# A hybrid decoder layer on one core: the projection's left operand turned by DMA instead of by TensorE

## The chip, the cores and the metric

The kernel runs on one core of a Trainium2 chip. The metric is the device time of one execution in microseconds (us). Each kernel is timed as the median of several executions, and one further execution was recorded by the hardware profiler; the rows shown here come from that recorded one. Engines are named as the profile names them: PE is TensorE, DVE is VectorE, ACT is ScalarE, POOL is GpSimd, SP is SyncE, which here only issues transfers. SPq in a row is SP's queue.

## The reference

One decoder layer over 4096 tokens of width 1024, in float32. The input is normed and projected to 2816 columns; 8 heads of windowed attention (window 128, with a sink and a slope per head) and 4 heads of a chunked linear recurrence run side by side on them. Each of the two gives 512 columns per token:

```python
attn = rmsnorm(swa_sink_alibi(q_a, k_a, v_a, attn_sinks[l]), attn_out_norm[l])
hg = hgrn2(q_h, f_h, i_h, lb_all[l])
hg = rmsnorm(hg, hgrn_out_norm[l].reshape(HGRN_HEADS, HGRN_VAL_DIM)).reshape(B, T, HGRN_WIDTH)
hg = hg * jax.nn.silu(g_h)
mix = jnp.concatenate([attn, hg], axis=-1) @ w_out[l]
x = x + ga1 * rmsnorm(mix, ln1_post[l])
```

Behind it stand a second norm, a router (4 groups, 8 experts in each, 2 experts per token) and the 32 experts' feed-forward, whose result is added to x after one more norm. The change concerns the operand of `@ w_out`, the "mixed heads".

## The kernel before

The kernel has three stages. The first sweep (to about 970 us of the trace) projects the tokens in 16 blocks of 256, runs the recurrence and leaves its 512 columns of each 128-token tile in DRAM (`hg_d`). The second sweep (about 970 to 1820 us) goes over 32 tiles of 128 tokens, two in a block: `g_qkv` projects queries, keys and values of a block, `g_attn` is the attention of one tile, `g_out` multiplies the mixed heads of one tile by `w_out`, `g_post` norms, adds, and makes the router's operand `h2T`, `g_route` routes four tiles at a time. The third stage runs the experts.

Products with a float32 operand are made of float16 halves: a value is scaled and split into a high part (rounded to float16) and a low part (the rest), and three matmuls, high by high, high by low and low by high, are summed in PSUM. The left operand of a matmul must lie transposed. In `g_out` (lines 1354 to 1386) the left operand is `mT`, 8 pieces of 128 columns with two halves each, so that a tile takes 2 x 8 x 3 = 48 matmuls of 128 x 512.

How `mT` is made before the change stands at the end of `g_attn` (lines 1336 to 1352). The tile's `mix` is 128 tokens x 1024 columns in float32: columns 0 to 511 are written by the attention, columns 512 to 1023 are loaded from `hg_d` at the beginning of `g_attn`. For each half of the columns TensorE turns four pieces of 128 x 128 in float32 into PSUM (`ps_t<-ident,mix`); ScalarE writes the scaled high half from PSUM, VectorE the low half. The recurrence's half goes first, the attention's half after its norm factor `r`, which VectorE multiplies in (`mix<-mix,rar`).

The order of the work is not written out by hand. `Weave` runs these functions as coroutines and keeps a model of the engines' clocks; it takes the next step of the first one whose operands should be there. So each engine's program, and SP's queue too, is the order in which the steps came up in that model, and it is fixed when the kernel is built. All loads and stores of the second sweep are issued by SP in that order, and SP waits at each transfer for what the transfer needs. `g_attn` of tile n starts once `mT` of tile n-2 was made (line 1237), and `mT` (two buffers) may be written once `g_out` of tile n-2 has ended (line 1341). One kind of DMA transpose is in the kernel already: `g_post` has SP turn the split router operand (`h2T<-x`, 128 x 2048 float16, 512 KB, 30 of them).

Of the kernel before, what the change touches and what calls it, by code (L numbers as in the profile page):

```python
# [9 lines left out]
F32 = mybir.dt.float32  # L10
F16 = mybir.dt.float16
FR = mybir.dt.float32r
BF = mybir.dt.bfloat16
# [3 lines left out]
AF = mybir.ActivationFunctionType  # L17
ALU = mybir.AluOpType
# [3 lines left out]
P = 128  # L22
D = 1024
KC = D // P
# [131 lines left out]
WAIT = "wait"  # L156
# [116 lines left out]
class Layer:  # L273
# [842 lines left out]
    def g_wo(self):  # L1116
# [4 lines left out]
        wo = self.wo = wp.tile([P, KC, 2, D], F16, name="w")  # L1121
# [20 lines left out]
    def sweep2(self, w16a):  # L1142
# [7 lines left out]
        with ExitStack() as ctx:  # L1150
# [23 lines left out]
            wr = op.tile([P, KC, 36], F32, name="mT")  # L1174
# [59 lines left out]
            def g_attn(n):  # L1234

                b, t = divmod(n, 2)
                while n >= 2 and ("mT", n - 2) not in st or ("q", b) not in st or n and ("s", n - 1) not in st:
                    yield WAIT
                qT, qv = st["q", b]
                mix = op.tile([P, D], F32, name="mix")  # L1240
                nc.sync.dma_start(mix[:, 512:], self.hg_d[n])
# [64 lines left out]
                mixa = mix[:, 0:512].rearrange("p (h d) -> p h d", d=64)  # L1306
# [29 lines left out]
                ss = sm.tile([P, 1], F32, name="ssa")  # L1336
                nc.scalar.activation(s[:, 0:2].rearrange("p h n -> p (h n)"), mix[:, 0:512], AF.Square,
                                     accum_out=ss)
                yield
                r = self.rstd(sm, ss, 1, 512, "ra")  # L1340
                while "const" not in st or n >= 2 and ("y", n - 2) not in st:
                    yield WAIT
                mT = op.tile([P, KC, 2, P], F16, name="mT")
                for kk in (1, 0):
                    if not kk:
                        yield [r]
                        nc.vector.tensor_scalar_mul(mix[:, 0:512], mix[:, 0:512], r)
                        yield
                    yield [mix, "ps_t"]
                    pt = ps_t.tile([P, 4, P], F32, name="ps_t")  # L1350
                    for k in range(4):
                        nc.tensor.transpose(pt[:, k], mix[:, (4 * kk + k) * P:(4 * kk + k + 1) * P], self.ident)
                    hi, lo2 = mT[:, 4 * kk:4 * kk + 4, 0], mT[:, 4 * kk:4 * kk + 4, 1]
                    nc.scalar.activation(hi, pt, AF.Copy, scale=osc[:, 1:2])
                    nc.vector.scalar_tensor_tensor(lo2, pt, osc[:, 1:2], hi, op0=ALU.mult, op1=ALU.subtract)
                st["mT", n] = mT

            def g_out(n):
                while ("mT", n) not in st or (n >= 3 and ("h2T", n - 3) not in st):
                    yield WAIT  # L1360
                mT = st["mT", n]
# [6 lines left out]
                yield [mT]  # L1368
                ym = xp.tile([P, D], F32, name="x", bufs=3)
                ss = sm.tile([P, 2], F32, name="ssy")  # L1370
                for c in range(2):
                    pj = ps_j.tile([P, 512], F32, name="ps_j")
                    for k in range(KC):
                        while ("wo", k) not in st:
                            yield WAIT
                        for i, (u, v) in enumerate(((0, 0), (0, 1), (1, 0))):
                            nc.tensor.matmul(pj, mT[:, k, v], wo[:, k, u, c * 512:(c + 1) * 512],
                                             start=(k == 0 and i == 0), stop=(k == KC - 1 and i == 2))
# [7 lines left out]
            def g_post(n):  # L1386
# [21 lines left out]
                if late:  # L1408
                    junk = op.tile([P, D], F32, name="mix")
# [911 lines left out]
```

## Time and profile before

| | |
|---|---|
| median of 3 runs (lowest, highest) | 2713.15 us (2712.32 to 2718.62) |
| the profiled execution: time, span | 2708.02 us, 2706.2 us |
| busy over the span | PE 92%, DVE 71%, ACT 50%, POOL 28% |
| second sweep, 1000 to 1800 us: busy | PE 95.4%, DVE 82.0%, ACT 55.5%, POOL 30.0% |
| second sweep: mean share of the 16 DMA engines | 0.45 |
| instructions on PE, matmuls | 19433 |

The span is the time from the first to the last instruction; the execution's own time lies 1.8 us above it. A row of groups gives the number of instructions, their busy time and the mean of one in nanoseconds, then the time that the engine sat idle just before them and what ended it. Matmuls are pipelined: the mean of one is its latency, so for a row of them the distance from one group's start to the next says more than the mean. All work is recorded under one line (L140, a helper), so groups are told apart by the names of their tiles.

### The profile page before, as it was taken

To read this page: it belongs to the slowest core of one execution; us is meant where nothing else is said; L and a number is where in the kernel's file an instruction comes from. 1 tells how busy PE (TensorE), PEld (TensorE's weight loads), DVE (VectorE), ACT (ScalarE), POOL (GpSimd) and SP (SyncE) were. 2 spreads that over 40 slices of the span, in tenths; PEclk is the share of its full clock that TensorE was granted. 3 is DMA by queue.
4 is the path that set the end of the run, shared out by engine and by line. 5 is a ranking of instruction groups with operands and counts; after the bars stand their busy time and mean duration, and the time that the engine had idled before them with its cause. 6 is when DMAs were issued, how large, how long until landed. Compare 5 with 4: busy or idle time off the path is not lost. (4 is left out here: it accounts for less than half of the span.)

```text
span 2706.2 us, 50271 instructions
## 1 busy us (share of the span) xinstructions
PE 2495.3 (92%) x19433; PEld 1908.5 (71%) x19433; DVE 1908.4 (71%) x4115; ACT 1360.0 (50%) x2932; POOL 758.8 (28%) x1075
## 2 busy tenths in 40 slices
PE   5989999999999989999999999975999989999992
PEld 2767667767766775766676667645998878888982
DVE  5657656787777678878788788884655656666774
ACT  4435544333433346546554655543555556666662
POOL 1111212211111001232332333334442333233336
PEclk8999999999999999999999999987999999999996
DMA  8212222222222243344446436536756878788988
GB/s 284 90 61 79 94 79 75 65 89 92 75 69 85 85 166 102 112 93 125 95 112 131 95 110 114 91 126 177 253 191 230 266 249 291 279 269 291 325 277 234
DMA packets 190602, 414.46 MB, mean 153 GB/s; under 512 B 85052, under 2 KB 120040, under 8 KB 168856
## 3 DMA queue, kind: packets, MB, share of 16 engines
q1 hardware_dynamic: 157360, 319.07, 37.8%
q0 software_dynamic: 31744, 91.60, 11.7%
q8 instruction: 153, 2.51, 0.4%
q14 instruction: 89, 0.73, 0.1%
q10 hardware_dynamic: 1256, 0.56, 0.1%
HBM read 284.60 MB, written 118.16 MB: 149 GB/s over the span
## 5 line engine op out<-in xcount | busy, mean ns | idle before, releaser
L140 PE MATMUL ps_g<-xT,w 128*128 128x256 f32 (+8 forms) x3072 | 465.5, 306 | 0.0
L140 PEld LDWEIGHTS ps_g<-xT,w 128*128 128x128 f32 x3072 | 436.1, 190 | 7.1 <-DVE xT L140 0.3
L140 PE MATMUL ps_j<-w,mT 128*128 128x512 f16 x1536 | 364.1, 381 | 0.0
L140 PE MATMUL ps_j<-hT,w 128*128 128x256 f16 x3072 | 348.7, 274 | 5.2 <-POOL hT L140 5.2
L140 PE MATMUL ps_j<-w,hT 128*128 128x512 f16 x1536 | 349.5, 380 | 0.0
L140 PEld LDWEIGHTS <-w 128*128 128x128 f16 x3072 | 301.8, 98 | 47.2 <-issue 8.7
L140 PEld LDWEIGHTS <-hT 128*128 128x128 f16 x2304 | 194.5, 98 | 164.0 <-issue 3.3
L140 PE MATMUL ps_d<-w,av 128*128 128x512 f32 (+6 forms) x1020 | 261.5, 401 | 4.6 <-ACT av L140 4.3
L140 ACT ACTIVATE w<-ws 128x512 fp32r<-128x512 f32 (+1 forms) x392 | 246.2, 678 | 29.7 <-DMA ws<-in_w_in_dram 25.1
L140 DVE TENSOR_TENSOR w<-ws,w 128x512 fp32r<-128x512 f32 x384 | 245.2, 685 | 2.1 <-ACT w L140 2.0
L140 PEld LDWEIGHTS <-mT 128*128 128x128 f16 x1536 | 143.3, 98 | 146.0 <-issue 8.6
L140 DVE TENSOR_TENSOR xT<-ps_x,xT 128x256 fp32r<-128x256 f32 (+8 forms) x256 | 115.2, 472 | 160.7 <-ACT xT L140 160.4
L140 PE MATMUL ps_j<-hT,w16a 128*128 128x256 f16 x1920 | 223.7, 276 | 0.0
L140 PEld LDWEIGHTS ps_d<-w,av 128*128 128x128 f32 (+6 forms) x1020 | 175.6, 178 | 53.8 <-ACT av L140 6.9
L140 PEld LDWEIGHTS <-w16a 128*128 128x128 f16 x1920 | 188.7, 99 | 26.4 <-issue 0.6
L140 POOL TENSOR_TENSOR hT<-hf,hT 128x512 f16<-128x512 f32 x64 | 103.6, 1619 | 269.8 <-ACT hT L140 255.3
L140 ACT ACTIVATE y<-ps_d,wgt 128x512 f32<-128x512 f32 (+4 forms) x141 | 97.1, 689 | 115.6 <-PE ps_d L140 92.1
L140 ACT ACTIVATE xT<-ps_x 128x256 fp32r<-128x256 f32 (+8 forms) x256 | 101.0, 422 | 103.7 <-PE ps_x L140 102.7
L140 ACT ACTIVATE s<-s,mx,qsc 128x256 f32<-128x256 f32 (+1 forms) x256 | 148.9, 584 | 0.0
L140 PE MATMUL ps_x<-ident,xg 128*128 128x128 f32 (+7 forms) x680 | 123.5, 289 | 26.7 <-DMA xg<-h_d,tok 16.0
L140 POOL DMA_INDIRECT xg<-h_d,tok x85 | 87.5, 1030 | 207.2 <-PE ps_x L140 187.7
L140 PEld LDWEIGHTS ps_x<-ident,xg 128*128 128x128 f32 (+7 forms) x680 | 104.6, 192 | 50.9 <-DMA xg<-h_d,tok 19.1
(405 smaller groups left out, 4243.4 us busy)
## 6 DMA issues: line engine op xcount, KB each, us to landing
ws<-in_w_exp_gate_dram SPq DMA_DIRECT2D x32, 1024.0 KB
ws<-in_w_exp_up_dram SPq DMA_DIRECT2D x32, 1024.0 KB
ws<-in_w_exp_down_dram SPq DMA_DIRECT2D x32, 1024.0 KB
yy<-y_d SPq DMA_DIRECT2D x24, 1024.0 KB
x<-in_x_dram SPq DMA_DIRECT2D x32, 512.0 KB
hT_d<-hT SPq DMA_DIRECT2D x16, 1024.0 KB
m_w<-in_w_ada_dram SPq DMA_DIRECT2D x128, 128.0 KB
hT<-hT_d SPq DMA_DIRECT2D x16, 1024.0 KB
```

The lines of the kernel that those rows point to most:

```text
L140: r = f(*a, **kw)
```

## The change

`mT` becomes two tiles of three buffers, `mT0` for the attention's half and `mT1` for the recurrence's. Each half is split while it still lies token by token: ScalarE writes the high part and VectorE the low part, both from SBUF, into 128 x 1024 float16 (`halves`), and SP turns that in one DMA transpose of 256 KB. The factor `r` is multiplied with the scale in one 128 x 1 operation (`rm`) and comes in as the scale of the split. The recurrence's half no longer lies in `mix`: it is loaded into `rec` and split by a coroutine of its own, `g_rec`. `halves` and `rec` lie in the half of the slot of `w` that `wo` does not take, which is free after the first sweep. `g_attn` of tile n now starts once `mT0` of n-3 and `mT1` of n-2 were made, and `g_out` takes the recurrence's pieces (4 to 7) first.

```diff
-        wo = self.wo = wp.tile([P, KC, 2, D], F16, name="w")
+        w = wp.tile([P, 2, KC * 2 * D], F16, name="w")
+        wo = self.wo = w[:, 0].rearrange("p (k u n) -> p k u n", k=KC, u=2)
+        self.halves = [[w[:, 1, c * D:(c + 1) * D].rearrange("p (u n) -> p u n", u=2) for c in (2 * i, 2 * i + 1)]
+                       for i in range(2)]
+        self.rec = [w[:, 1, c * D:(c + 1) * D].bitcast(F32) for c in (4, 5)]
...
-                while n >= 2 and ("mT", n - 2) not in st or ("q", b) not in st or n and ("s", n - 1) not in st:
+                while (n >= 3 and ("mT", n - 3, 0) not in st or n >= 2 and ("mT", n - 2, 1) not in st
+                       or ("q", b) not in st or n and ("s", n - 1) not in st):
...
-                mix = op.tile([P, D], F32, name="mix")
-                nc.sync.dma_start(mix[:, 512:], self.hg_d[n])
+                mix = op.tile([P, 512], F32, name="mix", bufs=3)
+                rec = self.rec[n % 2]
+                nc.sync.dma_start(rec, self.hg_d[n])
+                wv.add(g_rec(n, rec))
...
-                mT = op.tile([P, KC, 2, P], F16, name="mT")
-                for kk in (1, 0):
-                    if not kk:
-                        yield [r]
-                        nc.vector.tensor_scalar_mul(mix[:, 0:512], mix[:, 0:512], r)
-                        yield
-                    yield [mix, "ps_t"]
-                    pt = ps_t.tile([P, 4, P], F32, name="ps_t")
-                    for k in range(4):
-                        nc.tensor.transpose(pt[:, k], mix[:, (4 * kk + k) * P:(4 * kk + k + 1) * P], self.ident)
-                    hi, lo2 = mT[:, 4 * kk:4 * kk + 4, 0], mT[:, 4 * kk:4 * kk + 4, 1]
-                    nc.scalar.activation(hi, pt, AF.Copy, scale=osc[:, 1:2])
-                    nc.vector.scalar_tensor_tensor(lo2, pt, osc[:, 1:2], hi, op0=ALU.mult, op1=ALU.subtract)
-                st["mT", n] = mT
+                rm = sm.tile([P, 1], F32, name="rm", bufs=3)
+                nc.vector.tensor_mul(rm, r, osc[:, 1:2])
+                yield from turn(0, n, mix, rm)
+
+            def turn(i, n, x, scale):
+
+                while n >= 2 and ("mT", n - 2, i) not in st:
+                    yield WAIT
+                hl = self.halves[i][n % 2]
+                yield [scale, "Activation"]
+                nc.scalar.activation(hl[:, 0], x, AF.Copy, scale=scale)
+                yield
+                nc.vector.scalar_tensor_tensor(hl[:, 1], x, scale, hl[:, 0], op0=ALU.mult, op1=ALU.subtract)
+                while n >= 3 and ("y", n - 3) not in st:
+                    yield WAIT
+                yield
+                mT = op.tile([P, 2, 4, P], F16, name="mT%d" % i, bufs=3)
+                nc.sync.dma_start_transpose(mT.rearrange("p u k n -> p (u k) n"), hl.rearrange("p u n -> p (u n)"))
+                st["mT", n, i] = mT
```

In TensorE's program of before, in the middle of the second sweep, the four transposes of a half of the mixed heads stand between the projection's matmuls (`ps_j<-w,mT`) of an older tile and the transposes of the attention's weights `s`:

```order
L140 LDWEIGHTS mT
L140 MATMUL ps_j<-w,mT 128x512
L140 MATMUL ps_t<-ident,mix 128x128 x4
L140 MATMUL ps_t<-ident,s 128x128 x4
L140 LDWEIGHTS pT
L140 MATMUL ps_o<-iv,pT 128x128
```

In the changed program the same place reads so (the numbers behind `mT` are buffers):

```order
L140 LDWEIGHTS mT_17988
L140 MATMUL ps_j<-w,mT_17988 128x512
L140 MATMUL ps_t<-ident,s 128x128 x4
L140 LDWEIGHTS pT
L140 MATMUL ps_o<-iv,pT 128x128
```

The row with `mix` is gone, here and at all 64 such places; nothing has come in its stead on TensorE.

On SP, the stretch in which the attention of tiles 26 and 27 ends reads before as follows, where `xr` is the load of x for `g_post` of tiles 22 and 23, `out_0_dram` their result, `h2_d` the experts' input and `mix` the recurrence's half of tiles 28 and 29:

```order
L140 DMA xr_20590<-in_x_dram 128x1024
L140 DMA h2_d_111<-xr_20409 128x1024
L140 DMA out_0_dram<-x_20411 128x1024
L140 DMA h2_d_111<-xr_20590 128x1024
L140 DMA_TRANSPOSE h2T_20524<-x_20148 128x16x128
L140 DMA_TRANSPOSE h2T_20655<-x_20411 128x16x128
L140 DMA mix_20811<-hg_d28_87 128x512
L140 DMA mix_20959<-hg_d29_88 128x512
```

and in the changed program:

```order
L140 DMA out_0_dram<-x_19993 128x1024
L140 DMA h2_d_111<-xr_20233 128x1024
L140 DMA_TRANSPOSE mT0_20429<-w_10199 128x8x128
L140 DMA xr_20434<-in_x_dram 128x1024
L140 DMA_TRANSPOSE h2T_20325<-x_19993 128x16x128
L140 DMA out_0_dram<-x_20237 128x1024
L140 DMA_TRANSPOSE mT0_20544<-w_10199 128x8x128
L140 DMA h2_d_111<-xr_20434 128x1024
L140 DMA w_10199<-hg_d28_87 128x512
L140 DMA_TRANSPOSE h2T_20528<-x_20237 128x16x128
L140 DMA_TRANSPOSE mT1_20775<-w_10199 128x8x128
```

The transposes of `mT0` and `mT1` have come in between the loads and stores that stood there, two for each tile, one of them ahead of a load of x.

## Rows read from the trace of the kernel before

**Rows 1.** Three stretches: the second sweep's beginning, its body and its end. Behind a stretch and its length stand the busy times of PE, PEld, DVE, ACT and POOL with the numbers of instructions, TensorE's granted clock (1 is 2.4 GHz), the DMA engines' share and GB/s.

```profile
962.00:1000.00 38.00, 32.43 (x360) 28.23 (x360) 28.00 (x69) 20.12 (x62) 1.30 (x4) 0.87 0.47 156
1000.00:1800.00 800.00, 762.81 (x7071) 529.49 (x7070) 655.96 (x1555) 443.95 (x1172) 239.89 (x402) 0.99 0.45 109
1800.00:1830.00 30.00, 11.99 (x91) 8.57 (x89) 25.46 (x148) 7.54 (x18) 12.08 (x23) 0.61 0.49 172
```

**Rows 2.** Who waited for whom on TensorE from 1000 to 1800 us: total us, times, longest us.

```profile
PE ps_t L140 <- DVE mix L140: 12.9, 11, 4.8
PE ps_t L140 <- DVE pT L140: 7.5, 8, 1.8
PE ps_t L140 <- DVE big L140: 6.2, 5, 1.5
PE ps_s L140 <- DVE s L140: 4.9, 15, 0.5
PE ps_o L140 <- DVE mix L140: 3.2, 1, 3.2
```

**Rows 3.** The page's costliest groups, of TensorE: the projection by `w_out`, the projection of queries and values, the transposes of the mixed heads.

```profile
L140 PE MATMUL ps_j<-w,mT 128*128 128x512 f16 x1536 | 364.1, 381 | 0.0
L140 PE MATMUL ps_j<-hT,w16a 128*128 128x256 f16 x1920 | 223.7, 276 | 0.0
L140 PE MATMUL ps_t<-ident,mix 128*128 128x128 f32 x256 | 39.5, 278 | 20.6 <-DVE mix L140 12.9 <-DVE big L140 6.2 <-DVE pT L140 1.5
```

**Rows 4.** TensorE's instructions in order of time, merged: start, duration, and in brackets the idle time before.

```profile
1664.12 0.60 PE L140 MATMUL ps_t<-ident,mix 128*128 128x128 f32 x4
1664.56 0.62 PE L140 MATMUL ps_t<-ident,s 128*128 128x128 f32 x4
...
1668.07 0.81 PE L140 MATMUL ps_j<-w,mT 128*128 128x512 f16 x3
1669.59 0.63 PE L140 MATMUL ps_t<-ident,mix 128*128 128x128 f32 x4 [0.71 <-DVE mix L140]
1670.05 2.11 PE L140 MATMUL ps_j<-w,mT 128*128 128x512 f16 x9
...
1675.94 0.60 PE L140 MATMUL ps_t<-ident,mix 128*128 128x128 f32 x4
1676.38 2.78 PE L140 MATMUL ps_j<-hT,w16a 128*128 128x256 f16 x24
1680.66 0.63 PE L140 MATMUL ps_t<-ident,mix 128*128 128x128 f32 x4 [1.50 <-DVE big L140]
```

**Rows 5.** Groups of VectorE and ScalarE, from all the groups of the trace: those that the change removes or moves, and the nearest to what it adds.

```profile
L140 DVE SCALAR_TENSOR_TENSOR mT<-ps_t,qsc,mT 128x512 f16<-128x512 f32 x64 | 47.8, 747 | 22.7 <-ACT mT L140 22.4
L140 ACT ACTIVATE mT<-ps_t,qsc 128x512 f16<-128x512 f32 x64 | 43.8, 686 | 62.2 <-PE ps_t L140 62.0
L140 DVE TENSOR_SCALAR mix<-mix,rar 128x512 f32<-128x512 f32 x32 | 33.2, 1039 | 0.0
L140 DVE SCALAR_TENSOR_TENSOR x<-xr,rs,x 128x1024 f16<-128x1024 f32 x30 | 38.4, 1285 | 6.2 <-ACT x L140 6.2
L140 ACT ACTIVATE x<-xr,rs 128x1024 f16<-128x1024 f32 x30 | 34.4, 1146 | 17.3 <-DVE xr L140 11.1 <-issue 3.5 <-DMA out_dram<-x 2.5
L140 DVE TENSOR_TENSOR den<-den 128x8 f32<-128x8 f32 x64 | 10.3, 161 | 1.1
```

**Rows 6.** The issue of the DMA transposes that are there already: ns of SP (shortest, median, longest), first and last start.

```profile
L140 SPq DMA_TRANSPOSE h2T<-x x30: 1322/2472/8172, 1069.1 to 1803.8; - x30
```

**Rows 7.** Stretches with the columns of rows 1: 2.6 us in which one of these transposes ran, and 2.8 us of a plain load of 1 MB.

```profile
1524.90:1527.50 2.60, 2.60 (x26) 2.32 (x25) 1.67 (x3) 1.53 (x2) 2.16 (x5) 1.00 1.07 199
1486.60:1489.40 2.80, 2.80 (x14) 1.18 (x14) 2.69 (x10) 1.20 (x5) 2.36 (x5) 1.00 1.01 413
```

**Rows 8.** The DMA packets of the first of these two stretches.

```profile
DMA packets 2022, 0.52 MB, mean 199 GB/s; under 512 B 2022, under 2 KB 2022, under 8 KB 2022
```

**Rows 9.** The last such transpose whose landing was awaited, SP in order of time: start and duration of the issue.

```profile
1794.95 2.02 SPq L140 DMA_TRANSPOSE h2T<-x  x1
```

**Rows 10.** The router's matmuls that read it, TensorE in order of time.

```profile
1799.30 0.62 PE L140 MATMUL ps_s<-wr,h2T 128*128 128x72 f16 x16
```

**Rows 11.** What SP's queue waited for from 1100 to 1750 us, the three longest.

```profile
SPq L140 <- DVE x L140: 250.5, 30, 23.6
SPq L140 <- DVE mix L140: 63.9, 6, 18.1
SPq L140 <- DVE xr L140: 55.5, 7, 10.8
```

**Rows 12.** VectorE's wait for the load of x from 1000 to 1800 us.

```profile
DVE x L140 <- DMA xr<-in_x_dram: 13.5, 4, 5.7
```

More of the change, by code (lines that the diff above doesn't have):

```diff
@@ L1173, in sweep2 @@
             nc.sync.dma_start(sinkb, self.bcast(a["attn_sinks"], 8))
-            wr = op.tile([P, KC, 36], F32, name="mT")
+            wr = at.tile([P, KC, 36], F32, name="h2T", bufs=2)
             nc.sync.dma_start(wr[:, :, 0:4], a["w_router_group"][0].rearrange("(k p) n -> p k n", p=P))
@@ L1304, in tr @@
                     nc.vector.tensor_tensor(pT[g, kb][:, 1], pt, pT[g, kb][:, 0], op=ALU.subtract)
-                mixa = mix[:, 0:512].rearrange("p (h d) -> p h d", d=64)
+                mixa = mix.rearrange("p (h d) -> p h d", d=64)
                 def pv(g):
@@ L1335, in g_attn @@
                 yield
-                ss = sm.tile([P, 1], F32, name="ssa")
-                nc.scalar.activation(s[:, 0:2].rearrange("p h n -> p (h n)"), mix[:, 0:512], AF.Square,
+                ss = sm.tile([P, 1], F32, name="ssa", bufs=3)
+                nc.scalar.activation(s[:, 0:2].rearrange("p h n -> p (h n)"), mix, AF.Square,
                                      accum_out=ss)
                 yield
-                r = self.rstd(sm, ss, 1, 512, "ra")
-                while "const" not in st or n >= 2 and ("y", n - 2) not in st:
+                r = self.rstd(sm, ss, 1, 512, "ra", 3)
@@ L1342, in g_attn @@
+                while "const" not in st:
                     yield WAIT
[L1343 to L1355 removed]
@@ L1356, in g_attn @@
-                st["mT", n] = mT
+                yield
[12 more added lines that the diff above has]
+                    yield WAIT
+                yield
+                mT = op.tile([P, 2, 4, P], F16, name="mT%d" % i, bufs=3)
+                nc.sync.dma_start_transpose(mT.rearrange("p u k n -> p (u k) n"), hl.rearrange("p u n -> p (u n)"))
+                st["mT", n, i] = mT
@@ L1358, in g_out, with g_rec @@
+            def g_rec(n, rec):
+                while "const" not in st:
+                    yield WAIT
+                yield [rec]
+                yield from turn(1, n, rec, osc[:, 1:2])
             def g_out(n):
-                while ("mT", n) not in st or (n >= 3 and ("h2T", n - 3) not in st):
+                while ("mT", n, 0) not in st or ("mT", n, 1) not in st or (n >= 3 and ("h2T", n - 3) not in st):
                     yield WAIT
-                mT = st["mT", n]
+                mT = [st["mT", n, i] for i in range(2)]
@@ L1367, in g_out @@
                             nc.sync.dma_start(st["lx", i], a["x"][0, i * P:(i + 1) * P, :])
-                yield [mT]
+                yield mT
                 ym = xp.tile([P, D], F32, name="x", bufs=3)
@@ L1372, in g_out @@
                     pj = ps_j.tile([P, 512], F32, name="ps_j")
-                    for k in range(KC):
+                    for n8, k in enumerate((4, 5, 6, 7, 0, 1, 2, 3)):
                         while ("wo", k) not in st:
@@ L1376, in g_out @@
                         for i, (u, v) in enumerate(((0, 0), (0, 1), (1, 0))):
-                            nc.tensor.matmul(pj, mT[:, k, v], wo[:, k, u, c * 512:(c + 1) * 512],
-                                             start=(k == 0 and i == 0), stop=(k == KC - 1 and i == 2))
+                            nc.tensor.matmul(pj, mT[k // 4][:, v, k % 4], wo[:, k, u, c * 512:(c + 1) * 512],
+                                             start=(n8 == 0 and i == 0), stop=(n8 == KC - 1 and i == 2))
                         yield 0
@@ L1408, in g_post @@
                 if late:
-                    junk = op.tile([P, D], F32, name="mix")
+                    junk = op.tile([P, D], BF, name="mix", bufs=3)
                 else:
```

## The prediction

> **What bounds the kernel now.** I read the busy time by stretches first, because the change touches the second sweep alone. From 1000 to 1800 us TensorE is busy for 762.81 of 800 us at a granted clock of 0.99, VectorE for 655.96 (82%), ScalarE for 443.95, and the DMA engines have a share of 0.45 [rows 1]. So TensorE sets the pace there, VectorE is the next, and the DMA engines have half of their time free. The 37.2 us in which TensorE is idle are worth asking for one by one: in its list of waits the longest is for `mix`, 12.9 us, then for the low halves of the attention's weights and for the router's `big` [rows 2]. The groups of TensorE then say where such waits stand: 20.6 of the 37.2 us lie just before the transposes of the mixed heads [rows 3]. The order of time shows one case of each kind: a group of four transposes that runs straight through, one that begins 0.71 us late because VectorE has just written `mix`, and one that begins 1.50 us late behind the router's work on VectorE [rows 4]. These transposes are thus both work on the engine that sets the pace and the place at which it most often stands still.
>
> **TensorE, removed.** 32 tiles x 2 halves = 64 groups of four transposes go. The page's 39.5 us of busy time for them [rows 3] counts each group with its latency (0.60 us), but the next group starts 0.44 us after its beginning in the two undisturbed cases (1664.12 to 1664.56, 1675.94 to 1676.38), and 0.46 us in the third [rows 4]. I take 64 x 0.44 = 28.2 us and keep 39.5 us as the other bound. Nothing is added on TensorE; the projection's 48 matmuls per tile are the same with another order of pieces.
>
> **The waits before them.** 20.6 us end at these transposes. In the changed kernel no TensorE instruction waits for `mix` or for the factor `r`: the DMA transpose does. But VectorE's lateness itself is not gone, and the next instruction in TensorE's program that needs VectorE (the transposes of `s` need a free PSUM buffer, the scores need theirs read) may then stand still instead. Bounds are 0 and 20.6 us; no row says how much moves on, so I take the middle, 10.3 us.
>
> **VectorE and ScalarE.** VectorE loses 32 products of 128 x 512 at 1039 ns, 33.2 us. It gains 32 operations on one column, for which the nearest row is 161 ns: 5.2 us. The 64 low halves go from PSUM (747 ns) to SBUF; the nearest row, 128 x 1024 from SBUF into float16, takes 1285 ns, so half of it is 643 and with the size-independent part at most 747 ns: a gain of 0 to 6.7 us. ScalarE's 64 high halves go from 686 ns to something between 573 (half of 1146) and 686 ns [rows 5]. So VectorE falls by about 30 us, to 82% of a shorter sweep as before, and ScalarE stays where it is. I count neither as time, since neither sets the pace; what VectorE's relief could give is at most the 16.6 us of TensorE's other idle time, and I hold 0 to 5 us for it.
>
> **The transfers, added.** 64 transposes of 256 KB. One of 512 KB keeps all 16 DMA engines busy for 2.6 us, at 199 GB/s where a plain load in the row beside it moves 413 GB/s [rows 7], in packets all under 512 bytes [rows 8]. Half of it is 1.3 us, 64 times 83 us of the DMA engines, which lifts their share in the sweep from 0.45 to about 0.56. That is hidden as long as their landing is not awaited. A transpose of 512 KB was issued at 1794.95 and the matmuls that waited for it began at 1799.30 [rows 9, 10], 4.35 us; for half the size I subtract 1.3 us and get 3.0. In the changed program I counted the TensorE work between the issue of a tile's transpose and the first matmul that reads it, with the durations of the groups (364.1/1536 = 0.24 us for a matmul of 512 columns, 223.7/1920 = 0.12 for one of 256 [rows 3], the others likewise): in the body of the sweep never under 20 us, for most of the recurrence's halves about 55. Only for tile 2 at the beginning and for the attention's halves of the last two tiles it is 3 to 5 us. I add 3 us for these, bounds 0 and 10 (three places at which up to the whole 3 us is missed).
>
> **SP.** Each transpose takes SP about half of 2.47 us to issue [rows 6], 64 x 1.24 = 79 us in some 800. SP mostly waits: its three longest reasons alone make 370 of 650 us [rows 11]. What is queued behind a transpose of `mT0` or `mT1`, which waits for VectorE's low half, are the loads of x, the stores and the loads of `hT` a block ahead. The transpose is placed where the low half is expected to be ready, so I take 0 for this, and hold up to 75 us against it below.
>
> **The sum.** 28.2 + 10.3 - 3 = 35.5 us less. Against the profiled execution that is 2708.0 - 35.5 = 2672.5 us. That execution lies 5.1 us below the median of the runs (2713.15), and the changed kernel is compared with the median, so I forecast 2713.15 - 35.5, about 2678 us.
>
> **Rivals.**
> *The waits move and eat a part.* VectorE has 82% of the sweep and keeps it; if all 20.6 us of waits reappear at the scores and the transposes of `s`, and about 13 us of new standing still comes with the shorter sweep, 28.2 - 13 = 15 us are left: 2698 us. For it: all of TensorE's five longest waits are for VectorE [rows 2]. Against it: VectorE loses 30 us of work itself.
> *No change.* The pace is set by the chain of a tile (scores, softmax, weights, product, norm) and not by TensorE's total, so that freed TensorE time becomes idle time: 2708 to 2717 us. Against it speak the 95.4% of TensorE [rows 1]; the looser rule (three tiles ahead) shortens what hangs on that chain.
> *Slower: SP's queue.* SP issues in order, and one transpose of `mT0` stands ahead of a load of x in the changed order. If such a transpose waits, or its issue of 1.24 us and that of its sister (together 2.5 us) come ahead of that load in every tile, x lands 2.5 us later for 30 tiles, 75 us. VectorE already waited for that load four times, 13.5 us [rows 12]. If all of it fell on the path, the sum would be 75 - 38 = 37 us more, 2750 us; it decides from 38/30 = 1.3 us per tile on. Against it: g_post has slack behind that load, since the projection of the tile's second half and the norm factor come first, and VectorE still has 18% free. The Trainium skill stands on this side: "VectorE: DVE Perf Modes", section "Rules for kernel authors", would have a 128 x 128 transpose done by TensorE where PSUM will do as the destination, and by the crossbar DMA otherwise; PSUM did here, so by that rule the change goes the wrong way. The stretch in which TensorE is 95% and the DMA engines 45% busy speaks against applying it here, and no run of before tests it.
>
> **Chances and range.** The forecast 0.64, the part eaten 0.14, no change 0.10, slower 0.12. A change under 0.3% (8 us) is about what a measurement of this kernel cannot tell from none. The part eaten is faster by that bound but for a hundredth, so faster has 0.77, same 0.11, slower 0.12. The likeliest case's own range is 2656 (39.5 of work and 20.6 of waits less the 3 at the ends are 57) to 2693 (28.2 of work, no waits, less 8 at the ends, are 20). For 8 in 10 the range must reach into the part eaten and no change: 2656 to 2712.
>
> **What would show it.** TensorE should have no `ps_t<-ident,mix` group, and its busy time in the sweep should fall by about 28 to 40 us with its share still at 95% or above; the first sweep and the experts should take as long as before. If the waits moved, the list of TensorE's waits will show more for `s` and `pT`. If SP decides, VectorE's wait for the load of x will have grown from 13.5 us to some 70, and TensorE's share will have fallen below 92%. If a projection matmul waits for the transposes in the body of the sweep, for more than the few us at its ends, my count of 20 us of slack was wrong. The DMA share should be near 0.56; far above it, the transposes of half the size cost more than half.

## The result and the profile after

The changed kernel takes 2742.29 us (median of 6 runs, 2730.11 to 2753.26) where the kernel before takes 2711.50 (2708.18 to 2718.62): 1.0111 times as long, with an interval of 1.0096 to 1.0127. It is slower by 1.1%, and the forecast of 2678 us and its range were wrong. Its profiled execution took 2737.1 us with a span of 2735.3; before it was 2708.02 and 2706.2.

The same three stretches as in [rows 1], of the changed kernel:

```profile
962.00:1000.00 38.00, 32.46 (x342) 27.99 (x338) 20.49 (x52) 17.08 (x56) 1.18 (x3) 0.87 0.48 158
1000.00:1800.00 800.00, 729.05 (x6686) 497.36 (x6685) 637.16 (x1503) 433.63 (x1158) 246.21 (x383) 0.96 0.58 124
1800.00:1830.00 30.00, 27.31 (x158) 12.84 (x156) 26.72 (x83) 11.37 (x23) 12.96 (x20) 1.00 0.70 183
```

In the body TensorE is busy for 729 of 800 us instead of 763, VectorE and ScalarE have fallen too, the granted clock is 0.96 instead of 0.99, and at 1800 us the sweep is not over. No engine has become the bound: TensorE, VectorE and ScalarE all do less in the same time. So the next thing to ask for is who waits. Of the page's groups, those that answer to [rows 3] and the router's matmuls:

```profile
L140 PE MATMUL ps_j<-w,mT 128*128 128x512 f16 x1536 | 372.8, 390 | 3.9 <-DMA mT<-w 3.9
L140 PE MATMUL ps_j<-hT,w16a 128*128 128x256 f16 x1920 | 218.8, 275 | 5.5 <-DMA hT<-hT_d 5.5
L140 PE MATMUL ps_s<-wr,h2T 128*128 128x72 f16 (+1 forms) x512 | 23.2, 198 | 41.1 <-DVE s L140 36.8 <-DVE h2T L140 2.5 <-DVE hT L140 0.6
```

The group `ps_t<-ident,mix` is gone with its 20.6 us of idle time, and the projection hardly waits for the transposes (3.9 us). But before the router's matmuls TensorE now stands still for 41.1 us, where before the change it was 11.4 us:

```profile
L140 PE MATMUL ps_s<-wr,h2T 128*128 128x72 f16 (+1 forms) x512 | 21.3, 189 | 11.4 <-DMA h2T<-x 5.4 <-DVE s L140 3.4 <-DVE h2T L140 2.3
```

These matmuls now wait for VectorE to read scores out of the PSUM buffer that they need (`DVE s`). Who waits for whom on TensorE, against [rows 2], and on ScalarE, 1000 to 1800 us:

```profile
PE ps_s L140 <- DVE s L140: 44.3, 11, 7.6
PE ps_s L140 <- DVE mm L140: 6.7, 6, 1.7
PE ps_t L140 <- DVE pT L140: 6.6, 7, 1.7
```

```profile
ACT w L140 <- DMA w<-hg_d: 73.9, 18, 10.4
```

The second is the root, and one stall shows how it gets to TensorE. SP, ScalarE, VectorE and TensorE of the changed kernel in order of time:

```profile
1210.59 1.46 SPq L140 DMA_TRANSPOSE mT<-w  x1
1212.16 0.51 SPq L140 DMA_DIRECT2D h_d<-xr  x1
1213.52 5.94 SPq L140 DMA_TRANSPOSE h2T<-x  x1
1219.51 0.57 SPq L140 DMA_DIRECT2D w<-hg_d  x1
```

```profile
1214.49 0.28 ACT L140 ACTIVATE iv<-ps_j 128x128 f16<-128x128 f32 x1 [1.96 <-PE ps_j L140]
1224.40 0.72 ACT L140 ACTIVATE w<-w,qsc 128x512 f16<-128x512 f32 x1 [9.63 <-DMA w<-hg_d]
1225.02 0.26 ACT L140 ACTIVATE iv<-ps_j 128x128 f16<-128x128 f32 x1
```

```profile
1216.99 1.65 DVE L140 SCALAR_TENSOR_TENSOR s<-distm,slope,ps_s 128x256 f32<-128x256 f32 x4
1225.31 0.29 DVE L140 SCALAR_TENSOR_TENSOR iv<-ps_j,iv 128x128 f16<-128x128 f32 x1 [6.67 <-ACT iv L140]
...
1228.13 1.65 DVE L140 SCALAR_TENSOR_TENSOR s<-distm,slope,ps_s 128x256 f32<-128x256 f32 x4
```

```profile
1219.45 2.76 PE L140 MATMUL ps_j<-w,mT 128*128 128x512 f16 x12
1229.05 0.88 PE L140 MATMUL ps_s<-wr,h2T 128*128 128x72 f16 x16 [6.83 <-DVE s L140]
```

Read it from SP down. The load of the recurrence's half (`w<-hg_d`) stands on SP behind two transposes; the second takes 5.94 us to issue, and the load goes out at 1219.51. ScalarE's program has the split of that half (`w<-w,qsc`) next since 1214.8 and stands until 1224.40. Behind it waits ScalarE's high half `iv`, for that VectorE (6.67 us), behind that VectorE's reading of the scores, and for that TensorE (6.83 us). ScalarE waits for this load 18 times, about once per block. TensorE comes to stand still in every second block, where the router's matmuls need their scores read: six waits of 4.4 to 7.6 us, some 110 us apart, each along with one of ScalarE's six longest, make 34.6 of the 44.3 us. Another 7.3 us lie before the first projection by `w_out`.

Before the change the loads for the block's two tiles stood at nearly the same place of SP's queue, the first ahead of the long transpose and 7.8 us earlier than now, the second behind it:

```profile
1211.68 0.38 SPq L140 DMA_DIRECT2D mix<-hg_d  x1
1212.15 7.23 SPq L140 DMA_TRANSPOSE h2T<-x  x1
1219.48 0.53 SPq L140 DMA_DIRECT2D hT<-hT_d  x1
1220.06 1.40 SPq L140 DMA_DIRECT2D mix<-hg_d  x1
```

But there the half was read by TensorE at the end of the tile (the next such transposes after these loads begin at 1241.02), and nobody waited for it: the trace of before has no wait for `hg_d` at all. What the change moved above all is the reader, from the tile's end to its beginning. And what delays the load most in this case is a transpose of the router's operand, which was there before (7.23 us), and not one of the added ones.

Where the time went shows best if the body is cut from the first to the last matmul of the output projection. Before, and then after:

```profile
1013.00:1802.10 789.10, 751.91 (x6932) 518.99 (x6930) 646.75 (x1535) 439.86 (x1164) 237.46 (x366) 0.99 0.45 107
```

```profile
1021.50:1829.10 807.60, 741.80 (x6682) 498.70 (x6681) 643.72 (x1541) 437.25 (x1163) 256.31 (x366) 0.96 0.59 126
```

The spans differ by 29.1 us: the body begins 8.5 us later, takes 18.5 us more, the stretch from there to the first transposes of the experts' rows takes 1.5 less (1853.5 less 1802.1 against 1879.0 less 1829.1), and the experts take 3.6 more. In the body TensorE's busy time fell by only 10.1 us though 250 recorded matmuls are gone, since more of it ran at the lower of the two clocks, and its idle time rose from 37.2 to 65.8 us.

The clock was lost at the same places. In the 7 us behind the wait shown above the granted clock is 0.50, the lower of TensorE's two levels (1.2 GHz), and nine matmuls of the projection take 4.02 us there, where twelve took 2.76 us before the wait:

```profile
1229.05:1236.05 7.00, 7.00 (x43) 3.37 (x43) 4.43 (x10) 4.88 (x17) 0.00 (x0) 0.50 0.19 66
```

```profile
1231.96 4.02 PE L140 MATMUL ps_j<-w,mT 128*128 128x512 f16 x9
```

In each of the six long waits the granted clock fell to 0.50 before the wait was over and stayed there for 7 to 10 us.

### The profile page after: what moved, and what is told of

Its sections match the earlier page's. It is cut to its first block, busy times and chain, and to the rows that moved or that the text cites. A ratio compares the mean times of both kernels' runs of the same rounds, so it can differ in the third digit from the quotient of the medians.

```text
span 2735.3 us, 49851 instructions
## 1 busy us (share of the span) xinstructions
PE 2487.4 (91%) x19177; PEld 1887.9 (69%) x19177; DVE 1904.0 (70%) x4115; ACT 1356.6 (50%) x2932; POOL 779.5 (28%) x1075
## 5 line engine op out<-in xcount | busy, mean ns | idle before, releaser
L140 PE MATMUL ps_j<-w,mT 128*128 128x512 f16 x1536 | 372.8, 390 | 3.9 <-DMA mT<-w 3.9
```

The lines of the kernel that those rows point to most:

```text
L140: r = f(*a, **kw)
```

## The experiments

The theories: **A**, ScalarE stands in program order on a load that SP issues late, because the load is behind transposes on SP. **B**, the 64 added transfers crowd the DMA engines or SP. **C**, the new order and the looser rule of run-ahead are bad in themselves. The kernel before was run beside each of four sets; its medians there were 2728.7, 2731.0, 2709.8 and 2734.5 us on different chips, so kernels are compared by their ratio to it. The ratio is the one on record, with its interval; the quotient of the two medians differs from it by up to 0.0023 (0.9895 for e7).

**First set: one cure, one dose, one part.** e1 places the split later:

```diff
+                yield 12000.0
                 yield [rec]
                 yield from turn(1, n, rec, osc[:, 1:2])
```

> The changed kernel, with one line more: the split of the recurrence's half is placed 12 us later in the model's time, so that its load has 12 us more to land before ScalarE comes to it. Theory A (ScalarE stands in order at that split until a late load has landed, VectorE and TensorE stand behind it): ScalarE's wait for that load falls from 73.9 us to under 15, TensorE's wait for the scores from 44.3 to under 15, and the time falls by 35 to 45 us, to about 2700. Theory B (the 64 transposes crowd the DMA engines and SP's queue, whoever waits): 2730 to 2750 as now. Theory C (the new order with its run-ahead of three tiles is the cost): no fall either, 2730 to 2750.

Measured: 2725.57 us, 0.9984 (0.9971 to 0.9997). The wait for `hg_d` is gone from ScalarE's largest, but its place is taken in part by a new one on TensorE:

```profile
PE ps_j L140 <- DMA mT<-w: 16.8, 3, 11.8
PE ps_s L140 <- DVE s L140: 12.6, 19, 2.3
```

The ratio is 0.0127 below the changed kernel's 1.0111, some 35 us, the least that A expected. A is supported, not proven: with one step placed later, TensorE's matmuls come in another order over long stretches of the trace, so this kernel differs in more than the wait.

e2 leaves the order of the computation nearly as it is and issues the load two tiles earlier, into four buffers:

```diff
-        self.rec = [w[:, 1, c * D:(c + 1) * D].bitcast(F32) for c in (4, 5)]
+        self.rec = [w[:, 1, c * D:(c + 1) * D].bitcast(F32) for c in (4, 5, 6, 7)]
...
-                rec = self.rec[n % 2]
-                nc.sync.dma_start(rec, self.hg_d[n])
+                rec = self.rec[n % 4]
+                for i in range(0 if n == 0 else n + 2, min(n + 3, NT)):
+                    nc.sync.dma_start(self.rec[i % 4], self.hg_d[i])
```

> The changed kernel with four buffers for the recurrence's half and its load issued two tiles (some 50 us) earlier; the order on ScalarE, VectorE and TensorE stays nearly as it is, only SP's changes. Theory A (ScalarE stands at the split until the late load has landed): the wait of 73.9 us falls to under 5, TensorE's for the scores to under 15, time about 2700. Theory B (the transposes crowd DMA engines and SP): 2730 to 2750. Theory C (the order and the run-ahead): 2730 to 2750, since the compute engines' order is the same.

Measured: 2710.59 us, 0.9932 (0.9908 to 0.9957), faster than the kernel before. ScalarE does not wait for the load at all, and the body takes 769.2 us at a clock of 0.99:

```profile
L140 ACT ACTIVATE w<-w,qsc 128x512 f16<-128x512 f32 x32 | 22.8, 716 | 0.0
```

```profile
1020.90:1790.10 769.20, 726.95 (x6682) 493.68 (x6681) 643.99 (x1541) 435.59 (x1163) 256.48 (x366) 0.99 0.60 132
```

The last figures are the DMA engines' share and GB/s: 0.60 and 132, more than in the changed kernel. B does not go with that, nor does C, whose rule and order are all there.

e3 gives the kernel before the transfers alone: two transposes of 256 KB per tile that nobody reads.

```diff
                 st["mT", n] = mT
+                for i in range(2):
+                    nc.sync.dma_start_transpose(
+                        self.idle[1 + 2 * (n % 2) + i].rearrange("p (k n) -> p k n", n=P), self.idle[0])
```

> The kernel before, with two DMA transposes of 256 KB more in every tile that nothing waits for (their source is a region set to zero once, their result is not read), issued where the tile's left operand has been made. It measures what the 64 transfers cost by themselves, on the DMA engines and in SP's queue. Theory A: 2711 to 2717, as before, since no engine waits. Theory B: 2735 to 2750, most of the change's loss. Theory C: 2711 to 2717.

Measured: 2720.73 us, 0.9962 (0.9947 to 0.9977). The share in 1020 to 1800 us rises to 0.57 and nothing is lost:

```profile
1020.00:1800.00 780.00, 739.45 (x6835) 513.17 (x6833) 643.75 (x1497) 431.76 (x1142) 235.45 (x357) 0.99 0.57 129
```

B falls as the cause. That the kernel is even 0.4% faster than the kernel before is not explained.

e4 lets TensorE transpose the recurrence's half at the tile's end as before, and turns the attention's half alone by DMA:

```diff
-                wv.add(g_rec(n, rec))
...
+                yield [rec, "ps_t"]
+                pt = ps_t.tile([P, 4, P], F32, name="ps_t")
+                for k in range(4):
+                    nc.tensor.transpose(pt[:, k], rec[:, k * P:(k + 1) * P], self.ident)
+                mT1 = op.tile([P, 2, 4, P], F16, name="mT1", bufs=3)
+                nc.scalar.activation(mT1[:, 0], pt, AF.Copy, scale=osc[:, 1:2])
+                nc.vector.scalar_tensor_tensor(mT1[:, 1], pt, osc[:, 1:2], mT1[:, 0], op0=ALU.mult, op1=ALU.subtract)
```

> Half of the change: the attention's half is split and turned by DMA, the recurrence's half is turned by TensorE at the end of the tile's attention as before (32 groups of four transposes instead of 64), with the run-ahead of three tiles for the attention's half. ScalarE no longer has an instruction that reads the load early. Theory A: faster than before by about half of 28 to 38 us, 2692 to 2700. Theory B: half of the loss, about 2727. Theory C: slower than before by most of the loss, 2730 or more.

Measured: 2724.14 us, 0.9981 (0.9968 to 0.9993). Half of the change, with the urgent load taken out of it, costs nothing and gains next to nothing. A had expected 14 to 19 us less, so this is a miss; why half of the change brings so little stays open.

**Second set: the queue itself.** The changed kernel and the kernel before again, as controls on one chip:

> The changed kernel as it is, once more, on the chip of the other runs of this call, as their control. Every theory expects the ratio to the kernel before that it had: 1.0096 to 1.0127. Its stretch 1020:1800 should again show TensorE busy near 716 us.

> The kernel before, profiled on the chip of the other runs of this call, so that each stage of the other kernels has a stage of before on the same chip beside it. If the experts' stage (from the first transposes of their gathered rows to the end) takes as long here as in the other runs (865 us), the 10 us by which it was longer than in the first profile of before belong to the chip; if it takes 853 to 856 us, they belong to what the changed kernels leave behind at the end of the attention stage.

The changed kernel: 2746.14 us, 1.0044 (1.0027 to 1.0060); slower again, by less than the first time. The kernel before was profiled at 2725.93 us. Their bodies, before and after:

```profile
1010.10:1817.50 807.40, 758.99 (x6932) 522.27 (x6930) 647.55 (x1535) 439.31 (x1164) 237.18 (x366) 0.99 0.43 105
```

```profile
1020.70:1831.10 810.40, 746.84 (x6682) 499.54 (x6681) 643.06 (x1541) 436.63 (x1163) 256.31 (x366) 0.96 0.58 126
```

On this chip the bodies differ by only 3.0 us; of the 19.0 us by which the changed kernel's span is longer, 10.6 lie before the body and 6.4 in the experts. The chip gave the kernel before a body 18 us longer than its first profile, 11 of them idle, and the changed kernel one 3 us longer; I did not find out why. The experts' stage takes 855.5 us here before and 861.9 after, and 855.3 to 869.4 in the other kernels of the study, which don't touch it; since e7 alone shows 867.1 and, run again, 859.5, a difference of 8 us in this stage says nothing.

e7 changes one word of the changed kernel. The load is issued by GpSimd at the same place of the program; the instructions of TensorE, VectorE and ScalarE come in the same order in both traces:

```diff
-                nc.sync.dma_start(rec, self.hg_d[n])
+                nc.gpsimd.dma_start(rec, self.hg_d[n])
```

> The changed kernel with one word changed: the load of the recurrence's half is issued by GpSimd, at the same place of the program, so that it does not stand on SP's queue behind the transposes. Theory A (the load is late because its issue stands on SP behind transposes that wait for their splits) expects the gain of e2: a ratio of 0.993 to 0.997, no wait of ScalarE for this load among its largest (73.9 us in the changed kernel), TensorE busy 730 us or more in 1020:1800. A rival (the load is issued too late in the program as well, or GpSimd's own queue holds it up) expects that ScalarE still waits 40 us or more for it and a ratio above 1.003.

Measured: 2702.30 us, 0.9872 (0.9840 to 0.9904), faster than the 0.993 to 0.997 expected. Against the changed kernel of the same set that is 43.8 us for one queue. The body, ScalarE's split, and the place that was shown above, in e7:

```profile
1019.90:1785.60 765.70, 728.07 (x6682) 493.50 (x6681) 641.91 (x1542) 435.74 (x1163) 268.35 (x394) 0.99 0.63 133
```

```profile
L140 ACT ACTIVATE w<-w,qsc 128x512 f16<-128x512 f32 x32 | 22.9, 718 | 14.1 <-DMA w<-hg_d 13.5 <-issue 0.7
```

```profile
1207.70 0.62 POOL L140 DMA_DIRECT2D w<-hg_d  x1
```

```profile
1212.11 0.72 ACT L140 ACTIVATE w<-w,qsc 128x512 f16<-128x512 f32 x1 [0.76 <-DMA w<-hg_d]
```

The load goes out at 1207.70 instead of 1219.51, and ScalarE waits 0.76 us instead of 9.63. From the load's issue to the split it is 4.4 us here and 4.9 in the changed kernel, so it was the issue that was late and not the transfer that was slow. TensorE's wait for the scores to be read, from 1020 to 1800 us, in the changed kernel of this set and then in e7:

```profile
PE ps_s L140 <- DVE s L140: 30.9, 21, 6.5
```

```profile
PE ps_s L140 <- DVE s L140: 3.6, 7, 2.6
```

The transposes still stand on SP and still wait there (`DVE w`, the low halves, 190.4 us on SP from 1100 to 1750 us; 212.4 in the changed kernel). A is shown: same order, same transfers, same run-ahead, only the load is not behind them. The Trainium skill, "DMA: Bandwidth & Descriptors", section "Issuing engines are not separate DMA queues", says that a second issuing engine saves only the time of issuing, which is usually small. Here the load's own issue is 0.57 us, and the measurement differs from the rule: what the second queue saved was the waits of others that stand ahead on the first.

e6 is e2 with the old run-ahead rule:

```diff
-                while (n >= 3 and ("mT", n - 3, 0) not in st or n >= 2 and ("mT", n - 2, 1) not in st
+                while (n >= 2 and ("mT", n - 2, 0) not in st or n >= 2 and ("mT", n - 2, 1) not in st
```

> The kernel whose loads of the recurrence's half are issued two tiles earlier (e2), with the old rule of run-ahead for attention: a tile may begin only when the tile two before it has been turned (both halves). If attention's reach of three tiles is worth something, this kernel is slower than e2's 0.9932 (ratio to the kernel before), near 0.998, with TensorE's waits for the scores' reading (ps_s) above the 13.5 us of e2. If it was part of what made the changed kernel slower (theory C), it is faster than e2: below 0.990. If it decides nothing, 0.991 to 0.996.

Measured: 2714.69 us, 0.9937 (0.9915 to 0.9960), as e2 (0.9932). The order of TensorE hardly changes with the rule. Since e2 ran on another chip, and the changed kernel's ratio differed by 0.007 between two chips, this run alone could not show a small effect of the rule; C falls as the cause by e2 and e7, which have the looser rule and the new order and are faster than the kernel before.

**Third set: more cure, and the start.** e7 again (0.9921, 0.9890 to 0.9952, 2686.45 us, just outside the 0.980 to 0.991 expected), and e7 with e2's early issue:

> The kernel whose load of the recurrence's half is issued by GpSimd (e7), once more, as the control of this call, since the ratio of one kernel to the kernel before has differed by 0.007 between chips (1.0111 and 1.0044 for the changed kernel). Theory A expects it faster than the kernel before again, 0.980 to 0.991; a gain that belonged to one chip alone would give 0.995 or more.

> Both cures at once: the load of the recurrence's half issued two tiles earlier and by GpSimd. If the load's lateness is all that either cure removes (theory A), the second adds nothing: a ratio within 0.003 of the control of this call. If a load that is a little late still costs in the control, it is lower by more than 0.003.

Measured for the second: 2686.98 us, 0.9911 (0.9884 to 0.9938). Two cures are worth what one is, as A has it. The body of e7's second run:

```profile
1021.30:1776.30 755.00, 726.07 (x6681) 492.90 (x6681) 642.11 (x1541) 436.61 (x1163) 268.88 (x394) 0.99 0.63 135
```

e8 is e7 with the first tile's attention half transposed on TensorE again, and e12 with that of every tile; both carry one more condition, that attention waits for the squares of the tile two before:

```diff
             def turn(i, n, x, scale):
...
+                if n == 0 and i == 0:
...
+                        nc.vector.tensor_scalar_mul(x, x, scale)
...
+                        nc.tensor.transpose(pt[:, k], x[:, k * P:(k + 1) * P], self.ident)
```

> The control with the attention half of the first tile alone transposed by TensorE again, scaled before and split behind it (four transposes of 0.44 us, one multiplication). If the 8 to 11 us by which the output projection's first matmul is late in all changed kernels (1018.0 to 1021.5 against 1010.1 and 1013.0 in the kernel before) come of the way of the first tile's attention half through split, SP and DMA, it begins by 1013 us and the time falls by 5 to 10 us (a ratio 0.002 to 0.004 below the control). If they come of the loads and the constants around it, it begins at 1017 us or later and the time is the control's.

> The counterpart of e4: in every tile the attention half is transposed by TensorE (128 of the 256 transposes, about 14 us of work) and the recurrence half turned by DMA with its load issued by GpSimd. If each half turned by DMA is worth the work it takes off TensorE, it stands halfway between the kernel before and the control: 0.991 to 0.996. If the attention half's longer way by DMA costs more than it saves, it is as fast as the control or faster. If it is at 0.998 or above (as e4), TensorE's transposes between the attention's end and the projection bring their own waits back (the wait before ps_t for VectorE's mix, 13 us in the kernel before).

Measured: e8 2729.11 us, 1.0056 (1.0032 to 1.0079), first projection at 1017.5 us; e12 2736.12 us, 1.0091 (1.0064 to 1.0117), first projection at 1018.2. Both miss what I expected: the first was to be faster, the second to stand halfway. In e12 the old wait is back, the third of its cases and worse:

```profile
PE ps_t L140 <- DVE mix L140: 19.1, 15, 3.6
```

In e8 the one step put elsewhere changed TensorE's order in many places and the body grew to 799.8 us (1017.5 to 1817.3). Which of the moves costs it stays open. From e7 to e8, on one chip, the ratio rises by 0.0135, as much as the change is worth in e7: a new order of the work can move the time by that.

**Fourth set: what was left of the sum.**

> The kernel with the load issued by GpSimd (e7) and one added condition: attention on a tile begins only when the squares of the tile two before it are summed. e8 and e12 carried this condition and were slow (1.0056 and 1.0091). If the condition is the cause of that, this kernel is slow too, 1.003 or more. If their new order of work is the cause, it runs as e7: 0.987 to 0.993.

e13 is e7 with the added condition alone. Measured: 2700.74 us, 0.9890 (0.9862 to 0.9919). TensorE's matmuls come in e7's order, and the condition is innocent: e8 was slow by its order, and e12 by that and by the transposes and waits that it puts back, which these runs don't tell apart.

e14 is e13 without the wait for a free VectorE before three constants, of which one is shown:

```diff
-                yield [A2, "DVE"]
+                yield [A2]
```

> The kernel of e13 with the constants of the attention stage (the scaling of mod and the two maxima, three operations) placed as soon as their data is there, without waiting for a gap on VectorE. If the late first projection (1018 to 1021 us, against 1010 to 1013 before the change) comes of these constants, behind which the splits of both first tiles stand, its first matmul begins 5 us or more earlier than in e13 and the time falls by 4 to 10 us (0.0015 to 0.004). If it comes of the way through split, SP and DMA itself, the start moves by under 3 us and the time stays.

Measured: 2715.61 us, 0.9918 (0.9887 to 0.9949). The last constant's operation on VectorE comes at 999.77 us instead of 1010.56, and the first projection only at 1016.4 instead of 1019.0, so placing the constants early brings 2.6 of the 9 us by which the start is late. TensorE's waits at the start of e13, 962 to 1022 us:

```profile
PE ps_s L140 <- DVE s L140: 7.3, 2, 6.2
PE ps_j L140 <- DMA hT<-hT_d: 5.7, 1, 5.7
```

The second is no loss: in e7 the projection of the next queries goes on behind it at 966.7 us, and in the second profile of before at 967.3, there behind 8.3 us of waits for scores. The first, 7.3 us, stands where before there were projection matmuls to do. The rest seems to be the longer way: in e7 the factor `rm` is there at 1011.98 and the first projection begins at 1019.93, while in the kernel before it is 4.8 us from the last group of transposes ahead of it (1005.32) to the projection (1010.10). I have not isolated this further.

e15 is the kernel before with its load of the recurrence's half issued by GpSimd:

```diff
-                nc.sync.dma_start(mix[:, 512:], self.hg_d[n])
+                nc.gpsimd.dma_start(mix[:, 512:], self.hg_d[n])
```

> The kernel before with nothing changed but that GpSimd issues the load of the recurrence's half. There the half is first read some 20 us after its load (issued at 1211.7 us, transposed at 1241.0 in the profile of before), so theory A expects no change: 0.997 to 1.003. If moving the load off SP is a gain of its own, whatever the split, this kernel gains a good part of e7's 0.8 to 1.3%: below 0.995.

Measured: 2728.40 us, 0.9974 (0.9960 to 0.9988). At most 0.4% comes with moving the load alone; e7's 0.8 to 1.3% is for the larger part the change, once the load is in time.

e16 has GpSimd issue the load of x too:

```diff
-                    nc.sync.dma_start(xt, a["x"][0, n * P:(n + 1) * P, :])
+                    nc.gpsimd.dma_start(xt, a["x"][0, n * P:(n + 1) * P, :])
```

> The kernel of e7 with the load of x for the residual issued by GpSimd as well. My slower rival had this load as what SP's waits delay. VectorE's wait for it is 19 us of the stage in e7 and TensorE has no wait that follows from it; theory A expects the time of e13 within 0.003. If this load is the next thing that SP holds up, VectorE's wait for xr goes and the ratio falls by more than 0.003.

Measured: 2696.72 us, 0.9871 (0.9845 to 0.9896), against 0.9890 for e13. VectorE's wait for this load falls from 18.7 to 10.0 us in 1020 to 1800 us, and the time cannot be told from e13's.

e7 and e16 are 0.8 to 1.3% faster than the kernel before; e7 differs from the changed kernel by one word.

## Why the prediction was wrong, point by point

**The step that failed** is the one on SP: "What is queued behind a transpose of `mT0` or `mT1` ... are the loads of x, the stores and the loads of `hT` a block ahead ... so I take 0 for this". The load of the recurrence's half was not in that list, and with "ScalarE stays where it is" I asked what ScalarE's new work takes and not what it waits for. Nor are the transposes issued without waiting: in the changed kernel SP waits for the low halves 42 times from 1100 to 1750 us.

```profile
SPq L140 <- DVE w L140: 212.4, 42, 15.0
```

e7 has nearly the same waits on SP (190.4 us) without the loss, so they cost only what stands behind them and is needed soon. ScalarE executes in order, so its split of that half is a wait for a load in the middle of the attention's chain; I counted the slack behind the transposes (20 us, which held: 3.9 us of waits) and not the slack of the operand before them, which was nil. Measured on one chip, the changed kernel against e7, it costs 44.7 us of body: 25.9 of idle time on TensorE (63.6 against 37.6) and 18.8 of longer busy time (746.84 against 728.07) for the same 6682 recorded matmuls, since the granted clock of the body is 0.96 instead of 0.99.

**The slower rival** had the mechanism, head-of-line waiting on SP, with the wrong victim. VectorE's wait for x grew from 13.5 to 17.8 us and not to 70, and with less of it e16 is not measurably faster than e13. That TensorE's share would fall below 92% if SP decides came true: 729.05 of 800 is 91.1%.

**The rival by which freed time becomes idle time** looks right at first sight (TensorE's idle time rose), but e7 refutes it: with the load in time the freed time is gained.

**The terms of the sum** stand, apart from the start. TensorE's work, 28.2 us: the body's busy time is 30.9 us less in e7 than in the kernel before on the same chip (758.99 against 728.07), and 25.8 less in e7's second run than in the first profile of before (751.91 against 726.1). The waits before the transposes, 10.3 us: idle time falls by 10.8 (48.4 to 37.6) and 8.3 us (37.2 to 28.9) in the same pairs (the second one from two different sets of runs). That is near the half of 20.6 us that was taken, but the half was a guess between two bounds, and by e8 a new order of the work can move more than that; that it is these waits that fell is not shown. The start, 3 us with bounds 0 and 10, was mis-sized: the first projection begins 8.5 us later in the changed kernel and 9.8 in e7, and the reason given (transfers awaited by tile 2 and at the end) does not account for it: all waits for the transposes make 3.9 us. With that corrected, 28.2 + 10.3 - 9 is about 30 us, 1.1%; e7 measured 1.3 and 0.8%. With the 44.7 us of the late load as well the sum is about 15 us slower than before; the changed kernel measured 0.4% (12 us) and 1.1% (30 us).

**VectorE and ScalarE** were sized too well, without harm. Groups of the changed kernel, against [rows 5], first VectorE, then ScalarE:

```profile
L140 DVE SCALAR_TENSOR_TENSOR w<-mix,rm,w 128x512 f16<-128x512 f32 x32 | 23.8, 745 | 0.0
L140 DVE SCALAR_TENSOR_TENSOR w<-w,qsc 128x512 f16<-128x512 f32 x32 | 23.7, 743 | 0.2 <-ACT w L140 0.2
L140 DVE TENSOR_TENSOR rm<-rar,qsc 128x1 f32<-128x1 f32 x32 | 17.6, 554 | 3.0 <-POOL rar L140 3.0
```

```profile
L140 ACT ACTIVATE w<-w,qsc 128x512 f16<-128x512 f32 x32 | 22.9, 720 | 73.9 <-DMA w<-hg_d 73.9
L140 ACT ACTIVATE w<-mix,rm 128x512 f16<-128x512 f32 x32 | 22.9, 718 | 20.4 <-DVE rm L140 20.4
```

The low half takes as long from SBUF as from PSUM (743 to 745 ns against 747), the high half longer (718 to 720 against 686), and the one-column product 554 ns on average against the 161 of the nearest row. That average comes of a few long ones, the median is 150 ns; why they are long I did not find out:

```profile
L140 DVE TENSOR_TENSOR rm<-rar,qsc x32: 146/150/2304, 1013.5 to 1809.1; 128x1 f32<-128x1 f32 x32
```

VectorE's relief is thus 33.2 - 17.6 = 15.6 us, not 30.

**The transfers** were right: the DMA share is 0.58 to 0.59 (0.56 expected), and the issue of one transpose is 1.28 us (1.24 expected):

```profile
L140 SPq DMA_TRANSPOSE mT<-w x64: 1232/1284/2509, 1014.5 to 1815.0; - x64
L140 SPq DMA_TRANSPOSE h2T<-x x30: 1317/2358/5944, 1078.5 to 1825.6; - x30
```

The Trainium skill's rule in "VectorE: DVE Perf Modes", section "Rules for kernel authors" (TensorE for a 128 x 128 transpose where PSUM will do), does not decide here: in e3 the added transfers cost no time that shows, and in e7 TensorE, which sets the pace, is busy for 26 to 31 us less.

## What to carry to other kernels

When an operand's reader moves from the end of a step to its beginning, ask where its load stands, on which queue and behind whose waits; a load that nobody waited for shows in no list of waits, and says nothing of how late it is. A queue that issues in order delays a load by every wait ahead of it, so a transfer that waits for a computation and a load that a computation waits for belong on different queues, or the load a few tiles earlier. And for each engine that executes in order, count the new things it waits for, not only its new work: one late operand on an engine that is 54% busy held up the one that sets the pace. Where the order of the work comes out of a model, a small edit can reorder it and move the time by as much as the change is worth (e8); compare kernels of one order, as the changed kernel and e7 are, before naming a cause.

## What the runs showed of the hardware that was not expected

SP took up to 5.94 us to issue a transpose of 512 KB in the changed kernel, with a median of 2.36 us, and up to 8.17 in the kernel before [rows 6]; what makes some so long is not shown. The late load is paid twice: the changed kernel's two profiles have 26 to 37 us more idle time in the body than e7's two (63.6 and 65.8 against 28.9 and 37.6), and with it goes a granted clock of 0.96 instead of 0.99, so that the same matmuls are busy for 14 to 21 us longer (741.8 and 746.8 against 726.1 and 728.1). In its first profile the clock fell to 0.50 in each of the six long waits of TensorE, which e7 does not have. That idle time alone does it is not shown: the kernel before kept 0.99 with 48.4 us idle, for the most part in shorter waits. And chips differ: the kernel before had medians from 2709.8 to 2734.5 us beside the four sets, and the changed kernel's ratio to it was 1.0111 on one and 1.0044 on another, with intervals that don't meet.
